# A three-mixer layer with its MLP: background weight sums paced by landed loads, and two gates moved into the first pair of the MLP

## The chip, the cores and the metric
The program runs on one core of a Trainium2 chip. The metric is device time in microseconds (us), the median of three runs. Lower is better.

## The reference, cut to what matters
One layer of a hybrid backbone for 512 latent and 128 context tokens of width 1024, all in fp32:

```
h = rms_norm(x, n1) * (1 + sc1) + sh1
h @ w_in                      -> three parallel mixers:
  A  windowed attention (8 heads, with a position bias)
  B  gated DeltaNet (4 heads, two directions)
  C  GLA (4 heads, two directions)
merged = sigmoid(m_a)*(o_a @ w_br[0]) + sigmoid(m_b)*(o_b @ w_br[1]) + sigmoid(m_c)*(o_c @ w_br[2])
x  = x + gt1 * (merged @ w_o)
h2 = rms_norm(x, n2) * (1 + sc2) + sh2
u_val, u_gate = split(dw_conv(h2 @ w_up, f_conv))     # depthwise, width 3, 2816 columns each
x  = x + gt2 * ((silu(u_gate) * u_val) @ w_down)
```

Outputs are the two token streams, the context's keys and values, and the final states of B and C.

## The kernel before, in words
The 640 tokens lie as columns, features in partitions. A product takes a 128-column tile of a weight matrix, splits it into a high and a low float32r part and makes three products (high by high, high by low, low by high). `plan` lists all weight tiles in the order of use. `W(key)` steps through it by an index `i`: it loads up to two entries ahead into a ring of three buffers `raw` (SP issues, L140 and L270), and splits one ahead (ScalarE copies to `wh`, L149, VectorE subtracts to `wl`, L150, two buffers each). Entries 0 to 39 are the input projections, 40 to 55 and 56 to 71 the merge columns and branch products of C and of B by turns (`m`, `br`), 72 to 79 the `m` of A, 80 to 87 its `br`, 88 to 95 `w_out`, 96 to 103 the plain up-projections of MLP tiles 0 to 3 (`uv` value, `ug` gate), then the rest of the MLP. While entries 40 to 79 are worked off, the turns of attention run between them: scores, bias, softmax and values.

**The weight sums.** MLP tiles 4 to 21 (blocks 1 to 5 of `FBLK`) are computed in pairs of half-products (`up_pair`), Strassen-like, which needs sums of quarter blocks of `w_up`. They are made by DMA alone, DRAM to DRAM with adding on the way: eight transfers for each block (`sum_steps`), each of 1 MB or 0.75 MB, 40 in all, issued by GpSimd (POOL) in program order (L250). POOL waits for a transfer on which the next one rests. In `W` one transfer is issued at each index of `STEP_AT`: 11 to 22, and 42 to 69. POOL also does small vector work: `rsq` (L344), moves of the solve in B (L968 to L998), the bias of attention scores (`bm`, L1413), and in the last branch product the sum that closes `merged` (L1310).

**Order.** Up to the MLP's pairs a scheduler sets each engine's order; in the pairs (`manual_schedule`) the order is that of the code for TensorE, VectorE and ScalarE.

**MLP.** Products of tile 0 and of `uv` 1 are made early. `up_tile(f)` does product, depthwise convolution (`conv`, L515 on ScalarE, four L517 on VectorE), `silu`, product with the value and split (`gated`). The calls are tiles 1, 2, 3, 0, between them `sums_h2(k)`, which makes and splits the sums of the right side (L1709 to L1712, L407, L408). Then 18 pairs: in `up_pair(f, dn)` the seven half-products of tile f go to PSUM tiles X, Y and Z; the gate of the tile before is finished between them (`prev`), and the down-products `dn` of the block before follow.

Of the kernel before, what the change touches and what calls it, by code (L numbers as in the profile page):

```python
# [58 lines left out]
def hybrid_step(ctx: ExitStack, tc: tile.TileContext, a: dict, o: list):  # L59
# [202 lines left out]
    STEP_AT = [*range(11, 23), *range(42, 42 + len(sum_q) - 12)]  # L262
# [32 lines left out]
    def W(key):  # L295
# [3 lines left out]
        if i in STEP_AT:  # L299
            sum_q.pop(0)()  # L300
# [3 lines left out]
        with tc.high_priority() if i else nullcontext():  # L304
# [1362 lines left out]
    def up_tile(f):  # L1667
        ys = {}

        for key, f2 in sorted((("uv", f), ("ug", NF + f)), key=lambda i: (i[0], f) in early):  # L1670
            ys[key] = ft()
            if (key, f) in early:
                src = early[key, f]
            else:
                w = W((key, f))
                if (key, f) == ("ug", 2):

                    ps = mtile(), mtile()
                    for k in range(KT):
                        for i, (ww, xx) in enumerate(((w[0], h2H), (w[0], h2L), (w[1], h2H))):  # L1680
                            for p_, cs in zip(ps, (L, R)):
                                PE.matmul(out=p_[:, :HALF], lhsT=ww[:, k, :], rhs=xx[:, k, cs],
                                          start=(k == 0 and i == 0), stop=(k == KT - 1 and i == 2))
                    src = ft()
                    for p_, cs in zip(ps, (L, R)):
                        S.copy(src[:, cs], p_[:, :HALF])
                    early[key, f] = src
                else:
                    ps = gtile()
                    gemm_b(ps, w, lambda k: h2H[:, k, :], lambda k: h2L[:, k, :], KT)  # L1690
                    src = body(ps)
                if (key, f) == ("ug", 3):
                    need_split(("st", f + 1, 0))
# [4 lines left out]
        fslots.extend(ys.values())  # L1698

# [22 lines left out]

    open_ = {}
    wds = [g[0] for g in plan if g[0][0] == "wd"]

    def up_pair(f, dn):
# [153 lines left out]
```

## Time and profile before

| | us |
|---|---|
| median of 3 runs | 1410.02 (1408.38 to 1410.82) |
| profiled execution | 1408.28 |
| its span | 1406.5 |
| TensorE busy | 1317.5 (94%) |
| VectorE busy | 878.7 (62%) |
| ScalarE busy | 575.9 (41%) |
| GpSimd busy | 204.1 (15%) |
| mean granted TensorE clock | 0.969 of full |

Busy times are sums over instructions; TensorE's are modelled at their ends. Idle time in brackets in a timeline row is what came before the instruction, with what ended it. A window's DMA share is the mean busy share of the core's 16 DMA engines.

### The profile page before, as it was taken

How to read it: one execution, taken by the hardware profiler on the slowest of the kernel's cores; microseconds unless marked ns; L12 is line 12 of the kernel's file. 1: busy time of each engine (PE TensorE's matmuls, PEld its weight loads, DVE VectorE, ACT ScalarE, POOL GpSimd, SP SyncE). 2: the span in 40 equal slices, each digit the busy share in tenths (PEclk: the TensorE clock that was granted, in tenths of full speed). 3: DMA queues.
4: the chain of work that ended last, by engine and by line, in shares of the span. 5: the costliest groups of instructions: out<-in, count | busy, mean ns of one | idle time of the engine just before them, and what ended most of it. 6: DMA issues, size and time to landing. Idle time of an engine off the chain costs nothing.

```text
span 1406.5 us, 26976 instructions
## 1 busy us (share of the span) xinstructions
PE 1317.5 (94%) x10985; PEld 1249.3 (89%) x10985; DVE 878.7 (62%) x1827; ACT 575.9 (41%) x1082; POOL 204.1 (15%) x228
## 2 busy tenths in 40 slices
PE   5999999998979895989999999999899999999998
PEld 4899889898868794978998889899799999999998
DVE  4675876775688752234333434457977777777784
ACT  4543324422575531133333332456544344443342
POOL 1011113402234322102332003210000000000000
PEclk9999999998989997999999999999899999999999
DMA  9624555733011149669885552522144334443424
GB/s 274 165 61 117 146 140 121 170 81 77 24 31 42 48 131 247 134 146 247 222 213 135 167 153 78 146 80 61 58 130 128 117 116 128 123 125 113 121 66 115
DMA packets 241359, 175.72 MB, mean 125 GB/s; under 512 B 22678, under 2 KB 226228, under 8 KB 241076
## 3 DMA queue, kind: packets, MB, share of 16 engines
q1 hardware_dynamic: 227571, 135.92, 34.7%
q0 software_dynamic: 13280, 37.75, 11.4%
q8 instruction: 87, 1.43, 0.4%
q10 hardware_dynamic: 384, 0.33, 0.1%
q14 instruction: 37, 0.30, 0.1%
HBM read 167.42 MB, written 44.30 MB: 151 GB/s over the span
## 4 chain that ended last, share of the span: by engine, by line
PE 75%; DVE 8%; DMA 5%; ACT 4%; POOL 3%; issue 2%; SPq 1%; ACTq 0%; POOLq 0%; DVEq 0%
PE g L374 41%; PE m L1735 11%; PE s L1735 5%; PE g L395 4%; DMA raw<-in_w_branch_dram 2%; PE s L622 2%; DMA wada<-in_w_ada_dram 1%; PE s L422 1%; DVE wl L150 1%; POOL ssn L344 1%; PE s L1448 1%; ACT wh L149 1%; DVE t L517 1%; PE s L1436 1%; PE m L1398 1%
## 5 line engine op out<-in xcount | busy, mean ns | idle before, releaser
L150 DVE TENSOR_TENSOR wl<-raw,wh 128x1024 fp32r<-128x1024 f32 (+1 forms) x176 | 193.1, 1097 | 199.9 <-ACT wh L149 190.4
L149 ACT CAST wh<-raw 128x1024 fp32r<-128x1024 f32 (+1 forms) x176 | 164.8, 944 | 301.2 <-PE g L374 168.5
L374 PE MATMUL g<-hH,wh 128*128 128x320 f32 x768 | 187.2, 323 | 11.7 <-ACT wh L149 10.1
L374 PE MATMUL g<-hL,wh 128*128 128x320 f32 x768 | 184.7, 319 | 0.6 <-DVE hL L470 0.6
L374 PE MATMUL g<-hH,wl 128*128 128x320 f32 x768 | 183.0, 317 | 0.0
L374 PEld LDWEIGHTS g<-hH,wh 128*128 128x128 f32 x768 | 129.4, 192 | 20.0 <-ACT wh L149 10.9
L374 PEld LDWEIGHTS g<-hL,wh 128*128 128x128 f32 x768 | 131.3, 192 | 3.2 <-issue 1.8
L374 PEld LDWEIGHTS g<-hH,wl 128*128 128x128 f32 x768 | 131.9, 192 | 2.0 <-issue 1.8
L374 PE MATMUL g<-r,whd 128*128 128x320 f32 x704 | 132.5, 310 | 1.1 <-DVE xa L1810 1.1
L374 PEld LDWEIGHTS g<-r,whd 128*128 128x128 f32 x704 | 110.4, 188 | 1.4 <-ACT t L1796 1.4
L1735 PE MATMUL m<-r,wh 128*128 128x320 f32 x432 | 96.7, 311 | 2.8 <-ACT r L407 1.8
L395 PE MATMUL g<-wh,hH 128*128 128x256 f32 x320 | 95.8, 299 | 3.4 <-DVE xb L730 3.4
L395 PE MATMUL g<-wl,hH 128*128 128x256 f32 x320 | 95.0, 297 | 0.0
L395 PE MATMUL g<-wh,hL 128*128 128x256 f32 x320 | 94.9, 296 | 0.0
L517 DVE SCALAR_TENSOR_TENSOR t<-t,fcols,t 128x127 f32<-128x127 f32 (+1 forms) x160 | 84.0, 548 | 10.3 <-ACT t L515 7.7
L374 PE MATMUL g<-r,wld 128*128 128x320 f32 x352 | 80.8, 311 | 1.0 <-DVE wld L150 1.0
L374 PE MATMUL g<-oz,wh 128*128 128x320 f32 x384 | 74.0, 314 | 6.1 <-ACT wh L149 4.9
L1735 PEld LDWEIGHTS m<-r,wh 128*128 128x128 f32 x432 | 72.3, 188 | 3.3 <-ACT r L407 2.1
L1810 DVE SCALAR_TENSOR_TENSOR xa<-g,modc,xa 128x512 f32<-128x512 f32 x96 | 48.4, 546 | 38.4 <-PE g L374 37.7
L395 PEld LDWEIGHTS g<-wh,hH 128*128 128x128 f32 x320 | 63.9, 200 | 5.2 <-DVE xb L730 3.6
L1735 PE MATMUL m<-r,wl 128*128 128x320 f32 x216 | 66.9, 310 | 0.0
L374 PEld LDWEIGHTS g<-oz,wh 128*128 128x128 f32 x384 | 60.1, 189 | 7.2 <-ACT wh L149 5.3
(602 smaller groups left out, 2881.4 us busy)
## 6 DMA issues: line engine op xcount, KB each, us to landing
raw<-in_w_in_dram SPq DMA_DIRECT2D x64, 512.0 KB
wsum<-in_w_up_dram POOLq DMA_DIRECT2D x18, 1024.0 KB, 10.8
raw<-wsum SPq DMA_DIRECT2D x72, 256.0 KB
wada<-in_w_ada_dram SPq DMA_DIRECT2D x32, 512.0 KB
raw<-in_w_up_dram SPq DMA_DIRECT2D x54, 256.0 KB
wsum<-in_w_up_dram POOLq DMA_DIRECT2D x12, 768.0 KB, 10.9
wat<-in_w_ada_dram SPq DMA_DIRECT2D x16, 512.0 KB
rawd<-in_w_down_dram SPq DMA_DIRECT2D x32, 256.0 KB
```

The source lines that it names most:

```text
L149: S.copy(wh[:, :m], raw[:, :m])
L150: V.tensor_sub(wl[:, :m], raw[:, :m], wh[:, :m].bitcast(F32))
L344: G.tensor_tensor(out=out, in0=out, in1=mh.broadcast_to([P, n]), op=ALU.pow)
L374: PE.matmul(out=ps[:, OFF + c0:OFF + c1], lhsT=ww[:, k, :], rhs=xx(k)[:, c0:c1], start=(k == 0 and i == 0), stop=(k == kt - 1 and i == 2))
L395: PE.matmul(out=ps[b][:, o:o + GRP], lhsT=xx[:, 4 * kh + k, cs], rhs=ww[:, k, :], start=(kh == 0 and c % 2 == 0 and k == 0 and i == 0), st ...
L422: PE.matmul(out=pa[32 * g:32 * g + 32, :w], lhsT=csil[:, k, :], rhs=t[g], start=start, stop=stop)
L517: V.scalar_tensor_tensor(out=y[:, o0:o1], in0=src[:, i0:i0 + o1 - o0], scalar=w3(t), in1=y[:, o0:o1], op0=ALU.mult, op1=ALU.add)
L622: PE.transpose(pt[:, i * P:(i + 1) * P], src[:, (c0 + i) * P:(c0 + i + 1) * P], ident)
L1398: PE.matmul(out=ps[:, 0:256], lhsT=qT_[t][b, qs], rhs=kT_[t][b, :TS].rearrange("p (r k) -> p r k", k=64)[:, :, CST[j]:CST[j] + 32], start= ...
L1436: PE.transpose(pt[:, i * P:(i + 1) * P], Pt[:, i * P:(i + 1) * P], ident)
L1735: PE.matmul(out=out, lhsT=ww[:, 4 * kh + k, :], rhs=xx(hl_, k), start=start and k == 0 and i == 0, stop=stop and k == 3 and i == 2, skip_g ...
L1810: V.scalar_tensor_tensor(out=x1[nt][:, c0:c1], in0=body(ps)[:, c0:c1], scalar=modc[:, 40 + nt, r:r + 1], in1=x1[nt][:, c0:c1], op0=ALU.mul ...
```

## The change
1. The 40 transfers of the sums are issued elsewhere. `SUM_AT` has 32 indices: 11 to 20, every second from 44 to 78, then 82, 86, 90 and 94. The last eight (block 5) are issued one in each of the first eight pairs.
2. Ahead of each transfer POOL copies one element of the `raw` buffer of that index to `tick`. POOL so waits until that load has landed, and the buffer can be loaded anew only after the copy.
3. Gate of tile 3 and both convolutions, gate and splits of tile 0 are taken out of `up_tile` and put into the first pair, as a list `gates`, between its half-products. `up_tile(3)` keeps the convolution of its value; the gate's product stays in PSUM until the pair.
4. Down-products of block 0 take their tiles in the order 1, 2, 3, 0.
5. The rest of the diff gives names to pieces that were there (`up_plain`, `gate_conv`, `gate_mul`, `gate_split` in place of `last_gate`).

```diff
-    STEP_AT = [*range(11, 23), *range(42, 42 + len(sum_q) - 12)]
+    SUM_AT = [*range(11, 21), *range(44, 80, 2), 82, 86, 90, 94]
+    tick = cp.tile([1, 1], F32, name="tick")
+    def sum_step(raw):
+        if sum_q:
+            G.tensor_copy(out=tick, in_=raw[0:1, 0:1])
+            sum_q.pop(0)()
...
-        if i in STEP_AT:
-            sum_q.pop(0)()
...
+        if i in SUM_AT:
+            sum_step(loaded[i])
         return split[i]
...
+        first = f == fst[1]
         u1, u2 = ft(), ft()
+        gates = open_.pop("gates", [])
...
+        if gates:
+            gate_conv(gates[0])
...
         V.tensor_add(u2[:, R], u2[:, L], Z)
+        if first:
+            gates[1][1] = conv_u(gates[1][1], gates[1][0])
         prod(X, w, 1, lambda j, k: hH2[j][:, 4 + k, L], False, True)
+        if gates:
+            gate_mul(gates[0])
...
         need_split(("st", f, 3))
+        sum_step(loaded[pidx["st", f, 3]])
...
+        if first:
+            V.tensor_sub(u2[:, R], Y, u2[:, R])
+            need_split(dn[0])
+            gate_conv(gates[1])
+            gate_mul(gates[1])
+        for g in gates:
+            gate_split(g)
...
+               ks=None if b else (1, 2, 3, 0))
...
-    up_tile(3)
+    y3 = ft()
+    conv(y3, up_plain("uv", 3), lambda tap: fcols[:, tap, 3:4])
     sums_h2(3)
-    up_tile(0)
+    open_["gates"] = [[3, y3, up_plain("ug", 3)], [0, early["uv", 0], early["ug", 0]]]
+    need_split(("st", fst[1], 0))
```

What this makes of the order on POOL where the turns of attention begin, before:

```order
L1371 MEMSET bm 128x1152
L250 DMA wsum_96<-wsum_95 16x16384
L250 DMA wsum_100<-wsum_99 16x16384
L1413 TENSOR_TENSOR bm<-Gt,wm 128x256 x2
L250 DMA wsum_96<-in_w_up_dram 512x512
L250 DMA wsum_100<-in_w_up_dram 512x512
L1413 TENSOR_TENSOR bm<-Gt,wm 128x256 x2
L250 DMA wsum_102<-in_w_up_dram 512x512
L250 DMA wsum_105<-in_w_up_dram 512x512
```

and now (`raw_6318` and `raw_6443` are the loads of entries 44 and 46, `raw_6587` that of 48):

```order
L1380 MEMSET bm 128x1152
L1422 TENSOR_TENSOR bm<-Gt,wm 128x256 x7
L268 COPY tick<-raw_6318 1x1
L250 DMA wsum_95<-in_w_up_dram 512x512
L268 COPY tick<-raw_6443 1x1
L250 DMA wsum_99<-in_w_up_dram 512x512
L1422 TENSOR_TENSOR bm<-Gt,wm 128x256 x2
L268 COPY tick<-raw_6587 1x1
L250 DMA wsum_96<-wsum_95 16x16384
```

Eight transfers stood ahead of the eighth `bm`; now two do, each behind a `tick`, and from there on two `bm` stand between one `tick` and the next or the one after.

The same queue in the last branch product, where each row of L1310 closes `merged` for one of eight tiles. Before, nothing stood between them:

```order
L1310 TENSOR_TENSOR xa_504<-xa_504,xb_516 128x640
L1310 TENSOR_TENSOR xb_524<-xb_524,xb_530 128x640
L1310 TENSOR_TENSOR xb_512<-xb_512,xb_527 128x640
L1310 TENSOR_TENSOR xa_505<-xa_505,xb_518 128x640
L1310 TENSOR_TENSOR xb_513<-xb_513,xb_522 128x640
```

and now (`raw_9450` is the load of entry 86, `raw_9639` that of 90):

```order
L1319 TENSOR_TENSOR xa_505<-xa_505,xb_517 128x640
L268 COPY tick<-raw_9450 1x1
L250 DMA wsum_108<-wsum_107 16x12288
L1319 TENSOR_TENSOR xb_525<-xb_525,xb_531 128x640
L1319 TENSOR_TENSOR xb_513<-xb_513,xb_528 128x640
L1319 TENSOR_TENSOR xa_506<-xa_506,xb_519 128x640
L1319 TENSOR_TENSOR xb_514<-xb_514,xb_523 128x640
L1319 TENSOR_TENSOR xb_512<-xb_512,xb_527 128x640
L268 COPY tick<-raw_9639 1x1
L250 DMA wsum_104<-in_w_up_dram 512x512
L1319 TENSOR_TENSOR xa_503<-xa_503,xb_518 128x640
```

A copy of a sum now stands between the second and the third tile, an adding transfer ahead of the eighth.

VectorE around the start of the first pair, before (`gx` rows make the last right sides, `t<-g` rows are convolutions of tile 3 out of PSUM, L1750 is the pair's first combination):

```order
L150 TENSOR_TENSOR wl_10808<-raw_10694,wh_10807 128x1024
L517 SCALAR_TENSOR_TENSOR t_9579<-g_10758,fcols,t_9579 128x511
L1709 TENSOR_TENSOR gx_9910<-gx_9910 128x320
...
L408 TENSOR_TENSOR r_9597<-gx_9910,r_9596 128x640
L408 TENSOR_TENSOR r_9599<-gx_10212,r_9598 128x640
L408 TENSOR_TENSOR r_9595<-t_9582,r_9594 128x640
...
L517 SCALAR_TENSOR_TENSOR t_9583<-t_9580,fcols,t_9583 128x511
L517 SCALAR_TENSOR_TENSOR t_9583<-t_9580,fcols,t_9583 128x127
L150 TENSOR_TENSOR wl_10881<-raw_10755,wh_10880 128x1024
L517 SCALAR_TENSOR_TENSOR t_9583<-t_9580,fcols,t_9583 128x127
L1750 TENSOR_TENSOR t_9584<-t_9582,m_10865 128x320
```

and now:

```order
L1718 TENSOR_TENSOR gx_9933<-gx_9933 128x320
L150 TENSOR_TENSOR wl_10845<-raw_10720,wh_10844 128x1024
L1719 TENSOR_TENSOR gx_9933<-gx_9933,gx_10237 128x320
L150 TENSOR_TENSOR wl_10882<-raw_10793,wh_10881 128x1024
L1720 TENSOR_TENSOR gx_10237<-gx_10237,gx_9933 128x320
L417 TENSOR_TENSOR r_9616<-gx_9933,r_9615 128x640
...
L526 SCALAR_TENSOR_TENSOR t_9604<-g_10792,fcols,t_9604 128x511 x2
L417 TENSOR_TENSOR r_9618<-gx_10237,r_9617 128x640
L526 SCALAR_TENSOR_TENSOR t_9604<-g_10792,fcols,t_9604 128x127 x2
L1780 TENSOR_TENSOR t_9600<-t_9602,m_10867 128x320
```

The eight rows of L517 that convolve tile 0 have left this stretch, and the second weight split of the pair stands ahead of the last right sides. Behind the pair's second combination there now stand eight convolution rows, two gate products and two splits in place of one product and one split.

## Rows read from the trace of the kernel before

**Rows 1.** The page: an engine's busy time.
```profile
PE 1317.5 (94%) x10985; PEld 1249.3 (89%) x10985; DVE 878.7 (62%) x1827; ACT 575.9 (41%) x1082; POOL 204.1 (15%) x228
```

**Rows 2.** Windows: start, end, length; busy us (instructions) by engine; clock, DMA share, GB/s.
```profile
525.00:560.00 35.00, 18.91 (x120) 15.12 (x118) 10.76 (x29) 6.09 (x14) 9.74 (x13) 0.79 0.95 257
665.00:700.00 35.00, 35.00 (x269) 33.10 (x268) 13.33 (x33) 12.22 (x27) 11.47 (x12) 1.00 0.91 246
542.00:556.00 14.00, 1.51 (x5) 1.03 (x4) 1.81 (x3) 1.28 (x3) 1.40 (x2) 0.61 0.88 311
556.00:570.00 14.00, 12.24 (x56) 11.03 (x57) 1.20 (x3) 2.20 (x5) 0.00 (x0) 0.66 0.37 108
```

**Rows 3.** DMA view of 520 to 560: packets, MB, share; issues, KB each, us to landing.
```profile
q0 software_dynamic: 2039, 7.28, 62.6%
q1 hardware_dynamic: 3317, 3.38, 31.0%
...
wsum<-in_w_up_dram POOLq DMA_DIRECT2D x4, 1024.0 KB, 13.7
```

**Rows 4.** Timeline of POOL, 520 to 560: start, length, instruction, count.
```profile
528.31 2.12 POOL L250 DMA_DIRECT2D wsum<-in_w_up_dram  x2
...
538.31 1.49 POOL L250 DMA_DIRECT2D wsum<-in_w_up_dram  x2
...
541.32 1.24 POOL L250 DMA_DIRECT2D wsum<-in_w_up_dram  x2
```

**Rows 5.** Timeline of SP's issues, 520 to 560.
```profile
525.25 0.86 SPq L140 DMA_DIRECT2D raw<-in_w_in_dram  x1
```

**Rows 6.** Timeline of ScalarE, 520 to 560.
```profile
549.85 1.04 ACT L149 CAST wh<-raw 128x1024 fp32r<-128x1024 f32 x1 [7.61 <-DMA raw<-in_w_in_dram]
```

**Rows 7.** Timeline of TensorE, 540 to 606.
```profile
550.95 0.90 PE L374 MATMUL g<-hH,wh 128*128 128x320 f32 x2 [8.88 <-ACT wh L149]
...
557.24 1.43 PE L374 MATMUL g<-oz,wh 128*128 128x320 f32 x4 [4.86 <-ACT wh L149]
...
602.05 1.28 PE L1448 MATMUL s<-PT,Vj 128*64 128x128 f32 x7 [5.08 <-ACT PT L1438]
```

**Rows 8.** Chain of waits over the span: start, length, what; two turns.
```profile
662.47 7.23 PE g L374 x48
...
676.11 7.23 PE g L374 x48
```

**Rows 9.** Timeline of TensorE, 140 to 158.
```profile
148.23 1.30 PE L1209 MATMUL s<-ident,xa 128*128 128x128 f32 x5 [1.14 <-DVE stmp L980]
```

**Rows 10.** Timeline of POOL: the solve of B; the last branch product.
```profile
187.62 1.45 POOL L998 COPY T<-XT 32x320 f32<-32x320 f32 x3 [4.80 <-DMA XT<-Xd]
...
857.15 1.95 POOL L1310 TENSOR_TENSOR xa<-xa,xb 128x640 f32<-128x640 f32 x1 [2.43 <-DVE xb L1309]
...
879.07 2.41 POOL L1310 TENSOR_TENSOR xb<-xb,xb 128x640 f32<-128x640 f32 x1 [2.49 <-DVE xb L1309]
```

**Rows 11.** Timeline of TensorE, 885 to 892.
```profile
890.52 1.33 PE L622 MATMUL s<-ident,t 128*128 128x128 f32 x5 [1.17 <-DMA t<-in_x_sample_dram]
```

**Rows 12.** Chain of waits, at the loads of x_sample.
```profile
885.41 5.06 DMA t<-in_x_sample_dram
```

**Rows 13.** Windows at the start of the pairs, and of a later pair.
```profile
990.00:1000.00 10.00, 10.00 (x71) 10.00 (x70) 10.00 (x19) 6.78 (x11) 0.00 (x0) 1.00 0.10 29
1000.00:1010.00 10.00, 9.07 (x61) 8.54 (x59) 9.70 (x19) 5.54 (x9) 0.00 (x0) 1.00 0.18 52
1010.00:1020.00 10.00, 4.48 (x13) 3.46 (x14) 9.16 (x16) 4.46 (x7) 0.00 (x0) 0.63 0.10 30
1020.00:1030.00 10.00, 10.00 (x59) 9.79 (x59) 6.51 (x10) 5.45 (x9) 0.00 (x0) 0.85 0.55 161
1040.00:1060.00 20.00, 20.00 (x137) 20.00 (x137) 15.49 (x26) 8.81 (x14) 0.00 (x0) 1.00 0.41 119
```

**Rows 14.** Timeline of VectorE, 1005 to 1035.
```profile
1028.77 2.19 DVE L517 SCALAR_TENSOR_TENSOR t<-t,fcols,t 128x511 f32<-128x511 f32 x4 [0.36 <-ACT t L515]
```

More of the change, by code (lines that the diff above doesn't have):

```diff
@@ L364, in hybrid_step, with gemm_p @@
     V.tensor_copy(cols[:, :16], pt[:, :16])
-    def gemm_p(ps, w, xh, xl, kt, step=2, more=0):
+    def gemm_p(ps, w, xh, xl, kt, step=2, more=0, ks=None):
         wh, wl = w
-        for k in range(kt):
-            if k and k % step == 0:
+        ks = ks or range(kt)
+        for n, k in enumerate(ks):
+            if n and n % step == 0:
                 yield
@@ L374, in gemm_p @@
                     PE.matmul(out=ps[:, OFF + c0:OFF + c1], lhsT=ww[:, k, :], rhs=xx(k)[:, c0:c1],
-                              start=(k == 0 and i == 0), stop=(k == kt - 1 and i == 2))
+                              start=(n == 0 and i == 0), stop=(n == kt - 1 and i == 2))
     def gemm_b(*args, **kw):
@@ L1673, in up_tile @@
                 src = early[key, f]
-            else:
[L1675 to L1693, printed above, removed]
+            elif (key, f) == ("ug", 2):
+                w = W((key, f))
+                ps = mtile(), mtile()
+                for k in range(KT):
+                    for i, (ww, xx) in enumerate(((w[0], h2H), (w[0], h2L), (w[1], h2H))):
+                        for p_, cs in zip(ps, (L, R)):
+                            PE.matmul(out=p_[:, :HALF], lhsT=ww[:, k, :], rhs=xx[:, k, cs],
+                                      start=(k == 0 and i == 0), stop=(k == KT - 1 and i == 2))
+                src = early[key, f] = ft()
+                for p_, cs in zip(ps, (L, R)):
+                    S.copy(src[:, cs], p_[:, :HALF])
+            else:
+                src = up_plain(key, f)
             conv(ys[key], src, lambda tap, f2=f2: fcols[:, tap, f2:f2 + 1])
@@ L1721, in conv_u, with gate_conv, gate_mul, gate_split @@
         return y
+    def gate_conv(g):
+        f, _, u = g
+        y = ft()
+        conv(y, u, lambda tap: fcols[:, tap, NF + f:NF + f + 1])
+        if f != 3:
+            fslots.append(u)
+        g[2] = y
+    def gate_mul(g):
+        S.activation(out=g[2], in_=g[2], func=AF.Silu)
+        V.tensor_mul(g[1], g[1], g[2])
+        fslots.append(g[2])
+    def gate_split(g):
+        ac[g[0]] = rt(2)
+        split_x(g[1], *(t[:, :T] for t in ac[g[0]]))
+        fslots.append(g[1])
     open_ = {}
@@ L1786, in up_pair @@
             if f == NF - 1 and i < 3:
[L1787 removed]
+                (gate_conv, gate_mul, gate_split)[i](open_["gates"][0])
             down(*key[1:])
             need_load(*wds[wds.index(key) + 2:wds.index(key) + 3])
[L1791 to L1800 removed]
     def down(b, nt):
```

36 lines of the change are left out of this document (10 added, 26 removed).

## The prediction

> **What bounds the kernel now.** I read the page first. TensorE is busy for 94% of the span, so time is won only where it idles or runs slowly [rows 1]. Then windows of equal length. Between 525 and 560 TensorE works 18.91 of 35 us, with the DMA engines at 0.95. Between 665 and 700 they are nearly as full (0.91), and TensorE works all 35 us [rows 2]. So full DMA engines alone do not stop it; what stops it is a load that lands too late.
>
> The DMA view of 520 to 560 says who filled them. The sums' queue (q0) takes 62.6% of 40 us, 25.0 us for 7.28 MB, and all other loads (q1) 31.0%, 12.4 us for 3.38 MB; four 1 MB sums took 13.7 us (median) to land [rows 3]. POOL issued six sums there, two at each of 528.31, 538.31 and 541.32 [rows 4]. The weight load of entry 42 was issued at 525.25 [rows 5], and ScalarE, which waited for it, began its copy at 549.85 [rows 6]: 24.6 us for 512 KB. TensorE stood 8.88 us for that copy, 4.86 us for the one after, and 5.08 us more at 602 behind a copy that also waited for its load [rows 7].
>
> **Term 1, the sums spaced out.** The six sums issued from 528 to 542 are gone from there: in the new order seven `bm` stand first, and the two sums then let through each follow a landed load, of entries 44 and 46. By the rates above, the loads of this stretch need 12.4 us of DMA time, and get it from 525 on; the load of entry 42 is then down well before TensorE is through with its earlier work at 542. What can go:
> - idle time, 8.88 + 4.86 + 5.08 = 18.8 us [rows 7];
> - slow work. The granted clock is 0.66 in the window from 556, so about 0.34 / 0.5 = 0.68 of its 14 us, 9.5 us, were at 1.2 GHz and not at 2.4, some 8 of them busy; with the 1.51 us of the window before, 9.4 us ran at half speed [rows 2] after TensorE had stood idle for 8.88 us. Half of that, 4.7 us, goes.
>
> Together 23.5 us. Slow work after the wait at 602 is not counted; I set it against waits that may stay. From above the term is 26 us, if that goes too and is half as long as the slow work counted. From below it is half, 12 us, if one sum in flight slows a load half as much as several do.
>
> From entry 44 on, a sum starts on every second entry, once in a turn of 676.11 - 662.47 = 13.6 us [rows 8], where before it was two. Between 665 and 700 those two and all loads moved 246 GB/s, 3.4 MB a turn, and TensorE never stood [rows 2]; with one sum of 1 MB less, 3.4 us less of DMA time at 25.0 / 7.28 us per MB, no new wait is counted.
>
> The Trainium skill speaks against this part: its page "DMA: Bandwidth & Descriptors", section "Rules for kernel authors", advises to issue a DMA early, compute, and wait for it late. By that, holding the sums back wins nothing, and the sum below would be 23.5 us higher. The trace disagrees for this stretch [rows 3, 5 to 7]: transfers needed only in the MLP were issued early, and loads needed at once came late.
>
> **Term 2, the sums' new places.** POOL works in order, so each `tick` holds what is behind it until a load has landed. Three places bear on the path.
> - Entry 14's `tick` stands before the second `rsq` of the keys. There TensorE waits 1.14 us already [rows 9]. 0 us if that load has landed by then; 3.4 us if the DMA time of one sum lies ahead of it. I take 1.
> - Ten sums now run up to entry 20, where before half of them came later. The solve's exchange through DRAM is among them: POOL's copies of `XT` wait 4.80 us for it [rows 10]. 0 to 4 us if a hop or two become half as long again; I take 2.
> - In the last branch product the chain runs through POOL: each L1310 takes 1.95 us and then waits 2.43 us for VectorE, which waits for ScalarE, which waits for the L1310 [rows 10]. The copy of a sum between the second and the third tile can wait for the load of entry 86, 0.5 us (0 to 2). The adding transfer ahead of the eighth tile fits into the 2.49 us gap, since issuing takes some 1.06 us [rows 4, 10]. But it runs into the loads of `x_sample`, for which TensorE waits 1.17 us [rows 11] and which is 5.06 us of the chain [rows 12]. It adds 3.4 us of DMA time beside them: 0 to 4 us, I take 2.5.
>
> The eight sums in the MLP cost nothing: POOL has no other work there, and a pair's window shows DMA at 0.41 of 20 us [rows 13], to which 0.75 MB adds 2.6 us. Block 5 is needed ten tiles later. Should that cover go, a pair would wait for about one landing, 13.7 us [rows 3]. The 40 `tick` copies themselves are of one element; I count them at nothing, since POOL idles 85% of the span.
>
> Term 2 costs 6.0 us, between 0 and 14.
>
> **Term 3, the gates.** VectorE is full from 990 (10.00, 9.70 and 9.16 of 10 us), and TensorE stands 0.93 + 5.52 = 6.45 us between 1000 and 1020 [rows 13]. It then runs slowly: granted 0.63 and 0.85 mean 7.4 and 3 us at 1.2 GHz. All of the 3 and about 3.5 of the 7.4 are busy, so 3.2 us are lost. At most 9.7 us can go.
>
> Tile 0's two convolutions leave that stretch, 2.19 us each [rows 14]. They come back inside the pair, with a gate product and splits, some 6 us more of VectorE work between the pair's first combination and the end of its half-products. TensorE has four half-products there, 48 matmuls, 7.2 us at the pace of the plain ones [rows 8], then a down-product whose last two tiles need exactly these gates. I followed both engines through the pair: the left side's last split comes out at most 1 us earlier than now, the second weight split some 8 us earlier, so the half-products end about 7 us earlier; the first down-product then waits for the splits of tiles 3 and 0 for about 2 us. That leaves 5 us, of which I take 4.5. VectorE, with 15.49 us of work in 20 us of a later pair [rows 13], catches up in the next one. From above 9.7; from below a loss of 4 us, if the 6 added us of VectorE come on the path with no earlier start. The order 1, 2, 3, 0 puts the late tiles last; alone it costs nothing, since the products are the same.
>
> **Sum.** 1408.28 - 23.5 + 6.0 - 4.5 = 1386.3 for the profiled execution. That lies 1.7 us under the median of 1410.02, so I expect a median of 1388.
>
> **Rivals.**
> - *A sum in flight slows the loads, however few there are.* In 520 to 560 the loads got half the time that the sums got [rows 3]. If each sum still delays the load behind it, half of term 1 stays and term 2 is nearer 8: 1410.0 - 12 + 8 - 4.5 = 1401.5. Against it: 665 to 700 [rows 2]. The page "DMA: Bandwidth & Descriptors", section "Queues, rings and completion order" of the Trainium skill has each DMA engine go round among its queues by packets; by that one queued sum takes as large a share as six, though for a shorter time. Chance 0.17.
> - *The first pair becomes VectorE's.* Term 3 turns into 4 us of loss: 1396.5. For it: 6 us of work more beside 7.2. Against it: TensorE was already waiting on that engine before. Chance 0.10.
> - *The `tick` becomes the new wait, and the kernel slower.* Behind each of the 18 `tick` of entries 44 to 78 stands `bm`, without which no turn of attention goes on, and the `raw` buffer is free only after it. This decides if a load takes longer than one turn, 13.6 us, to land; 24.6 us did occur [rows 5, 6]. Then some 2 us a turn in 16 turns, 32 us, outweigh 23.5 + 4.5 - 6.0: about 1420. Against it: that landing had six sums beside it, and now has one. Chance 0.05.
> - *The change does not space anything.* Loads run two entries ahead, so a `tick` can find its load landed and pass at once; the sums then bunch as before and the loads wait, with term 3 eaten by term 2: 1410. Against it: between `tick` pairs stand `bm` rows that go by turns. Chance 0.05.
>
> **The numbers.** The forecast, 1388, has the remaining 0.63. About 0.2%, 2.8 us, is what a measurement of this kernel tells from no change. The first two rivals are faster too: faster 0.90, same 0.05, slower 0.05. For the range, the forecast's own bounds give 1410.0 - 26 + 1 - 9.7 = 1375 below; above, the first rival with term 2 a little dearer, 1404. That leaves the last two rivals and a tail below outside.
>
> **What would show it.** Right: in the window of 35 us after the first `bm` TensorE is busy for more than 32 us at a clock near 1.00; no copy of ScalarE waits over 3 us for a `raw` load in entries 42 to 56; sums are about 13 us apart on POOL; at the start of the pairs TensorE idles for under 4 us. Term 2 is wrong if TensorE's wait for `x_sample` stays at 1.2 us, or grows beyond 5. The whole is wrong if `bm` waits for a `tick`, or if TensorE still waits for `wh` for over 10 us in all.

## The result, and the profile after

The changed kernel takes 1393.9 us, the median of four runs (1386.24 to 1396.34), beside 1409.2 us for the kernel before on the same chip: 0.989 of it, with a 95% interval of 0.985 to 0.9925. A second set of six runs, below, gave 1391.9 us and 0.990 (0.9875 to 0.993). The profiled execution took 1386.24 us, the fastest of its set.

The page, its line of busy times and the line of the sums' queue: TensorE has 9.6 us less busy time than in [rows 1], a share of 94% as before.

```profile
PE 1307.9 (94%) x10985; PEld 1241.0 (90%) x10985; DVE 877.2 (63%) x1827; ACT 575.7 (42%) x1082; POOL 211.1 (15%) x268
...
q0 software_dynamic: 13280, 37.75, 12.2%
```

The windows that answer to [rows 2]:

```profile
525.00:560.00 35.00, 32.01 (x215) 28.08 (x213) 14.35 (x35) 10.32 (x20) 6.35 (x9) 0.95 0.48 120
...
542.00:556.00 14.00, 11.80 (x71) 9.79 (x71) 5.46 (x17) 3.63 (x10) 2.50 (x5) 0.88 0.48 131
556.00:570.00 14.00, 14.00 (x100) 13.39 (x99) 4.72 (x7) 4.53 (x7) 2.41 (x4) 1.00 0.75 170
```

From 525 to 560 TensorE now works 32.01 us in place of 18.91, at a granted clock of 0.95 in place of 0.79, and the DMA engines are half empty. POOL's timeline in that stage answers to [rows 4]. Each row gives start, length, instruction, and in brackets the idle time before it and what ended it:

```profile
555.09 0.18 POOL L268 COPY tick<-raw 1x1 f32<-1x1 f32 x1 [9.72 <-DMA raw<-in_w_in_dram]
555.33 1.16 POOL L250 DMA_DIRECT2D wsum<-in_w_up_dram  x1
567.77 0.17 POOL L268 COPY tick<-raw 1x1 f32<-1x1 f32 x1 [11.28 <-DMA raw<-in_w_in_dram]
568.21 1.04 POOL L250 DMA_DIRECT2D wsum<-in_w_up_dram  x1 [0.27 <-issue]
```

One sum is issued at 555 and the next 13 us later, where six were issued from 528 to 542. But TensorE has new waits. The list of its waits over the span (us in total, times, longest):

```profile
PE m L1029 <- DMA XT<-Xd: 10.1, 2, 9.9
...
PE s L631 <- DMA t<-in_x_sample_dram: 5.7, 1, 5.7
...
PE g L383 <- ACT wh L149: 1.8, 2, 1.2
```

In the kernel before, the same list had

```profile
PE g L374 <- ACT wh L149: 15.0, 3, 8.9
```

The wait for `x_sample` was 1.17 us [rows 11], and those for `XT` were 0.4 us each; in exchange the 15.0 us for `wh` are down to 1.8. The next table is the main instrument of what follows; the kernels of its lower rows are explained below. It cuts the profiled execution of each kernel at the same ten instructions of TensorE, found in the timelines by their order. In the kernel before these lie at 161.1, 206.6, 527.5, 662.5, 772.6, 832.8, 891.9, 984.4, 1048.5 and 1397.6 us. Lengths in us; some 10.5 us follow the last.

| kernel | S1 start | S2 exchange of `XT` in B | S3 to the first merge product | S4 attention, merge of C | S5 merge of B | S6 `m` of A, first `br` | S7 last branch product, `x_sample` | S8 `w_out`, plain tiles | S9 first pairs | S10 rest |
|---|---|---|---|---|---|---|---|---|---|---|
| before | 161.1 | 45.5 | 320.9 | 135.0 | 110.2 | 60.2 | 59.0 | 92.6 | 64.1 | 349.1 |
| changed | 157.9 | 55.2 | 317.8 | 109.9 | 110.2 | 61.3 | 63.6 | 92.5 | 59.3 | 347.9 |
| again | 161.1 | 56.3 | 318.4 | 109.4 | 110.2 | 61.6 | 63.6 | 92.2 | 59.4 | 347.9 |
| sums_only | 162.4 | 55.9 | 318.2 | 111.2 | 110.2 | 61.6 | 63.5 | 91.6 | 63.9 | 349.1 |
| gates_only | 159.6 | 45.2 | 323.9 | 134.4 | 110.2 | 60.2 | 57.4 | 90.4 | 58.5 | 347.9 |
| xt_clear | 160.6 | 44.1 | 325.0 | 111.3 | 110.2 | 61.3 | 62.9 | 92.1 | 58.7 | 347.9 |
| xs_clear | 158.5 | 57.2 | 319.5 | 111.1 | 110.2 | 61.9 | 58.1 | 90.4 | 58.9 | 347.9 |
| no_tick | 159.8 | 45.1 | 321.1 | 114.2 | 110.2 | 65.9 | 58.9 | 90.4 | 59.1 | 347.9 |
| old_places | 158.2 | 57.0 | 316.1 | 128.1 | 113.1 | 60.2 | 57.3 | 90.4 | 58.6 | 347.9 |
| twice | 158.1 | 57.1 | 314.6 | 125.7 | 119.7 | 60.2 | 63.4 | 91.2 | 58.9 | 347.9 |
| clear_places | 157.6 | 44.4 | 322.6 | 111.2 | 110.2 | 61.4 | 57.8 | 91.2 | 58.9 | 347.9 |
| clear_late_tick | 161.1 | 45.3 | 317.3 | 111.3 | 110.2 | 61.1 | 57.8 | 91.4 | 64.4 | 347.9 |
| clear_mlp_tick | 159.7 | 45.2 | 320.6 | 111.3 | 110.2 | 61.7 | 58.1 | 90.9 | 58.7 | 348.0 |
| clear_no_tick | 157.3 | 46.7 | 322.6 | 113.6 | 110.2 | 67.3 | 57.2 | 90.5 | 63.6 | 347.9 |

Read the first two rows against each other: the change wins 25.1 us in S4, 4.8 in S9, 1.2 in S10, 3.2 in S1 and 3.1 in S3. It loses 9.7 in S2, 1.1 in S6 and 4.6 in S7. The sum is -22, the difference of the profiled times.

My theory after this: the gain of S4 is that of the sums spaced out; the losses of S2 and S7 are sums that now fly beside transfers on which TensorE waits at once. The rivals: those two waits have other causes; the wait for a landed load, and not the place, wins or loses; a sum slows loads however few there are.

### The profile page after: what moved, and what is told of

It reads as the page before. It is cut to its first block, busy times and chain, and to the rows that moved or that the text cites. A ratio compares the mean times of both kernels' runs of the same rounds, so it can differ in the third digit from the quotient of the medians.

```text
span 1384.5 us, 27048 instructions
## 1 busy us (share of the span) xinstructions
PE 1307.9 (94%) x10985; PEld 1241.0 (90%) x10985; DVE 877.2 (63%) x1827; ACT 575.7 (42%) x1082; POOL 211.1 (15%) x268
## 4 chain that ended last, share of the span: by engine, by line
PE 63%; DVE 7%; ACT 3%; POOL 3%; DMA 2%; issue 2%; SPq 0%; ACTq 0%; DVEq 0%; POOLq 0%
PE g L383 37%; PE m L1763 11%; PE s L1763 5%; PE s L431 1%; PE s L631 1%; PE g L404 1%; DVE wl L150 1%; PE s L1457 1%; PE s L1445 1%; POOL ssn L352 1%; DMA raw<-in_w_in_dram 1%; DMA t<-in_x_sample_dram 1%; PE m L1407 1%; POOL xb L1319 1%; PE m L1691 1%
## 5 line engine op out<-in xcount | busy, mean ns | idle before, releaser
L383 PEld LDWEIGHTS g<-hH,wh 128*128 128x128 f32 x768 | 128.7, 190 | 11.8 <-issue 3.9
L383 PEld LDWEIGHTS g<-r,whd 128*128 128x128 f32 x704 | 110.2, 188 | 2.1 <-ACT t L1742 1.4
L526 DVE SCALAR_TENSOR_TENSOR t<-t,fcols,t 128x511 f32<-128x511 f32 (+1 forms) x160 | 84.3, 548 | 10.4 <-ACT t L524 7.7
L404 PEld LDWEIGHTS g<-wh,hH 128*128 128x128 f32 x320 | 63.5, 199 | 5.2 <-DVE xb L739 3.6
L268 POOL COPY tick<-raw 1x1 f32<-1x1 f32 x40 | 8.4, 211 | 369.8 <-DMA raw<-in_w_up_dram 181.7
```

Source lines behind the costliest of these rows:

```text
L404: PE.matmul(out=ps[b][:, o:o + GRP], lhsT=xx[:, 4 * kh + k, cs], rhs=ww[:, k, :], start=(kh == 0 and c % 2 == 0 and k == 0 and i == 0), st ...
L526: V.scalar_tensor_tensor(out=y[:, o0:o1], in0=src[:, i0:i0 + o1 - o0], scalar=w3(t), in1=y[:, o0:o1], op0=ALU.mult, op1=ALU.add)
```

## Experiments: do the two parts, and the two new waits, come from where I think

**again** is the changed kernel itself.

> The changed kernel, unchanged, to see how far its runs lie apart. Theory: its executions lie between 1386 and 1397 us with a median near 1394, 0.988 to 0.990 of the kernel before. The profile shows again a wait of TensorE for XT (5 to 10 us) and for x_sample (4 to 6 us), and no wait for wh in entries 42 to 56. Rival: these two waits are chance and at least one of them is under 2 us in this profile; then the sums' new places did not cause them.

Measured: 1391.9 us (1387.0 to 1398.9). The profiled run took 1390.7 us. Both waits are there again; that for `XT` has split in two:

```profile
PE m L1030 <- DMA XT<-Xd: 6.2, 1, 6.2
...
PE s L631 <- DMA t<-in_x_sample_dram: 5.3, 1, 5.3
...
PE m L1029 <- DMA XT<-Xd: 3.3, 2, 3.1
```

So they are no accident. From the first profile this one differs by 4.5 us, of which 4.3 arise in S1 and S2; after that the two run in step. The expectation held for both waits; two of the six executions took longer than the 1397 us that I had named. What makes the executions of this kernel differ by 12 us in all was not tried.

**sums_only** has the sums of the changed kernel, and the gates as before: `up_tile(3)` and `up_tile(0)` whole, `prev` and `last_gate` in the pairs. Against the kernel before its edit is

```
-    STEP_AT = [*range(11, 23), *range(42, 42 + len(sum_q) - 12)]
+    SUM_AT = [*range(11, 21), *range(44, 80, 2), 82, 86, 90, 94]
...
-        if i in STEP_AT:
-            sum_q.pop(0)()
...
+        if i in SUM_AT:
+            sum_step(loaded[i])
...
         need_split(("st", f, 3))
+        sum_step(loaded[pidx["st", f, 3]])
```

> The sums' places and the tick of the changed kernel, the gates as before. Theory: the gates are worth 4.8 us of the change (from 968.47 to 1027.77 the changed kernel took 59.3 us, the one before 64.1), so this is 4.8 us slower than the changed kernel, about 1398.5, 0.992 of the kernel before, and the stretch from the first product of tile 4 to the downs of the second pair takes 64 us again. Rival: TensorE gives the gain back later in the MLP, where VectorE has to catch up: under 2 us apart.

Measured: 1394.3 us, 0.992 (0.990 to 0.993). S9 is 63.9 us, as before, and S10 349.1: against the changed kernel's 59.3 and 347.9 the gates are worth 5.8 us in the traces. The medians of this set lie only 2.4 us apart, less than the runs of one kernel do; the stretches carry the size, the medians only the direction.

**gates_only** is the other half: the changed kernel with the sums as before.

```
-    SUM_AT = [*range(11, 21), *range(44, 80, 2), 82, 86, 90, 94]
+    STEP_AT = [*range(11, 23), *range(42, 42 + len(sum_q) - 12)]
...
+        if i in STEP_AT:
+            sum_q.pop(0)()
...
-        if i in SUM_AT:
-            sum_step(loaded[i])
...
-        sum_step(loaded[pidx["st", f, 3]])
```

> The kernel before with the gates of tiles 3 and 0 in the first pair, the sums as before. Theory: the two parts don't touch each other, so the stretch from the first product of tile 4 to the downs of the second pair takes 59.3 us in place of 64.1 and the time falls by 4.8 us: 0.9966 of the kernel before. Rival: with the sums of block 1 long complete either way, nothing else can differ; but if the first pair waits for a split of a sum's load in this order, it is under 2 us.

Measured: 1398.5 us, 0.994 (0.992 to 0.9965). S4 stays at 134.4, S9 falls to 58.5 and S10 to 347.9: 6.8 us by these two stretches. The interval puts the whole at 5 to 12 us, more than I expected; S7 and S8 were 3.8 us shorter too in this execution, by 1.6 of them in S7, where the gates touch nothing. In the stretches the two parts are independent: S4 belongs to the sums, S9 and S10 to the gates. The medians do not add up as well: 11.9 us for the sums alone and 8.3 for the gates alone stand beside 14.3 for both, a difference at the edge of what the intervals allow.

**xt_clear** moves five sums.

```
-    SUM_AT = [*range(11, 21), *range(44, 80, 2), 82, 86, 90, 94]
+    SUM_AT = [*range(11, 16), *range(21, 26), *range(44, 80, 2), 82, 86, 90, 94]
```

> The changed kernel with the five sums of entries 16 to 20 moved to entries 21 to 25, where the DMA engines are busy for 0.13 of the time. Theory: the sums in flight slow the hops of Xd and XT through DRAM; without them the wait of 9.9 us at XT falls below 3 us, the products behind it come 6 to 7.6 us earlier, and 3 to 6 us of that are left at the end: about 1389.5, 0.9855 of the kernel before. Rival: the wait is that of VectorE's chain ahead of Xd, the sums have nothing to do with it: wait and time stay, 1394. A second rival: the new places cost the same in the stretch of entries 21 to 25, since POOL works for the states there and the tick holds it up: the wait goes, the time stays.

Measured: 1382.6 us, 0.983 (0.981 to 0.9845), 9 us better than the changed kernel by the medians, where I had 3 to 6. The profiled executions lie closer: this one is 6.1 us shorter than that of the repeat and 1.7 shorter than the first, so a part of the 9 us has no place in the traces. The wait at `XT` is gone and S2 is 44.1 us in place of 55.2. What a sum does to the exchange is in SP's issues. `XT` can be loaded only when `Xd` has landed in DRAM. In the changed kernel:

```profile
176.58 0.31 SPq L997 DMA_DIRECT2D Xd<-Y  x1
177.75 0.31 SPq L998 DMA_DIRECT2D Xd<-Uw  x1
184.26 0.32 SPq L1006 DMA_DIRECT2D XT<-Xd  x1
```

With the sums moved away:

```profile
178.84 0.31 SPq L997 DMA_DIRECT2D Xd<-Y  x1
180.02 0.31 SPq L998 DMA_DIRECT2D Xd<-Uw  x1
181.21 0.32 SPq L1006 DMA_DIRECT2D XT<-Xd  x1
```

The hop of 160 KB held the next one up for 7.7 us from its issue beside the sums, and for 2.4 without them. From 165 to 205 the sums' queue has a share of 57.9% in the changed kernel, and 5.8% here. The packets show how the delay comes about. In the changed kernel, from 177 to 182:

```profile
q0 software_dynamic: 374, 0.76, 82.4%
q1 hardware_dynamic: 375, 0.38, 28.5%
```

The two queues take turns, packet for packet. Those of q1 hold 1 KB here, while the hops', seen alone in xt_clear, hold 3.6 KB (0.27 MB in 76). So by their size they belong to the weight load issued ahead of the hop in the same queue: the sum slows that load, and the hop stands behind it.

The second rival has a part in it as well. S3 is 7.2 us longer than in the changed kernel. A part of that is slack: S3 is 314 to 320 us long in the kernels that have waited in S2, and 317 to 325 in the others. But some 4 us arise in one place, at the two sums of entries 24 and 25. In POOL's timeline their `tick` waits stand in front of the keys' `ssn`,

```profile
265.76 0.17 POOL L268 COPY tick<-raw 1x1 f32<-1x1 f32 x1 [1.28 <-DMA raw<-in_w_in_dram]
266.19 0.57 POOL L250 DMA_DIRECT2D wsum<-wsum  x1 [0.26 <-issue]
266.77 2.02 POOL L352 TENSOR_TENSOR ssn<-ssn,mh 128x10 f32<-128x10 f32 x1
```

and VectorE stands for it:

```profile
268.83 0.83 DVE L1207 TENSOR_TENSOR xa<-xa,ssn 128x640 f32<-128x640 f32 x1 [2.97 <-POOL ssn L352]
```

**xs_clear** leaves out the two last entries of the list, so two more sums fall to the MLP.

```
-    SUM_AT = [*range(11, 21), *range(44, 80, 2), 82, 86, 90, 94]
+    SUM_AT = [*range(11, 21), *range(44, 80, 2), 82, 86]
```

> The changed kernel without the sums of entries 90 and 94; all later sums move by two, and ten run in the MLP in place of eight. Theory: the sum issued at 861 us slows the loads of x_sample that start at 865; without it TensorE's wait of 5.7 us for x_sample falls to about 1.2 us, as before, and the time by 4.5 us: 1389.5, 0.9855 of the kernel before. The two more sums in the MLP cost nothing. Rival: the loads of x_sample compete with the w_out loads and not with the sum: the wait stays above 4 us, the time at 1394.

Measured: 1383.2 us, 0.9835 (0.982 to 0.985), nearly 9 us better than the changed kernel where I had 4.5. In the chain of waits the changed kernel has

```profile
864.91 9.62 DMA t<-in_x_sample_dram
```

and this one

```profile
871.71 4.07 DMA t<-in_x_sample_dram
```

The landing of 256 KB took 9.62 us beside a sum issued at 861.05, and 4.07 without; TensorE's wait fell by 5.5 us, and so did S7. Another 2.1 us are in S8, and there the clock differs. Windows of 17 us before and after the end of the wait, in the changed kernel

```profile
858.00:875.00 17.00, 8.93 (x53) 7.91 (x54) 8.26 (x15) 3.45 (x4) 6.00 (x4) 0.87 0.86 214
875.00:892.00 17.00, 17.00 (x103) 17.00 (x102) 5.66 (x7) 6.97 (x13) 2.83 (x3) 0.83 0.35 102
```

and in this one

```profile
858.60:875.60 17.00, 14.04 (x88) 12.59 (x86) 10.31 (x18) 5.93 (x8) 6.88 (x3) 1.00 0.62 180
876.00:893.00 17.00, 17.00 (x121) 16.99 (x121) 8.20 (x10) 8.68 (x17) 1.58 (x1) 1.00 0.49 143
```

Behind the longer wait TensorE worked all 17 us at a mean granted clock of 0.83, and did 103 instructions where it did 121 here. So a loss beyond the length of the wait went with it. That the wait caused it is not shown: in the kernel before the clock is 0.84 from 891 to 908 behind a wait of only 1.17 us, and S8 is as long, 92.6; in no_tick, below, it is 1.00 from 875 to 892 behind one of 1.7 us. The two more sums in the MLP cost nothing (S9 58.9, S10 347.9).

## Experiments: the wait for a landed load, and the rate

**no_tick** takes the copies away, and with them the wait.

```
         if sum_q:
-            G.tensor_copy(out=tick, in_=raw[0:1, 0:1])
             sum_q.pop(0)()
```

> The changed kernel without the copies of one element, so that no sum waits for a landed load; the sums stand at the same entries. Theory: in the attention stage the places do the work, since a bm of the turn stands between two sums on POOL; two sums start together at the beginning of it, then one a turn, and the 25 us that the stretch from 527.5 to 640.8 gained are lost by at most 5. In the first phase sums start earlier without the copies, so the wait at XT changes: below 6 us if they are through by then. Total 1385 to 1395, 0.985 to 0.992 of the kernel before. Rival: the wait for a landed load is what frees the loads; then TensorE waits for wh again for over 8 us and the stretch loses over 10: 1403 or more, 0.997.

Measured: 1382.7 us, 0.982 (0.9785 to 0.986): faster than the changed kernel by some 9 us, a little more than I expected of the theory. The stretches show a gain and a loss. S2 is 45.1 and S7 58.9; the wait at `XT` is gone, and that for `x_sample` is 1.7 us. A sum that reads no load is put by the scheduler behind other work of POOL, and so the sums happened to miss both places (two at 194.41, after the exchange; one at 860.06, 8.9 us ahead of the load of `x_sample`, and the next at 887.89). But S4 is 4.3 and S6 4.6 us longer. At the start of the attention stage three sums come close together,

```profile
523.10 1.16 POOL L250 DMA_DIRECT2D wsum<-in_w_up_dram  x1
...
536.79 1.00 POOL L250 DMA_DIRECT2D wsum<-in_w_up_dram  x1
...
540.42 0.56 POOL L250 DMA_DIRECT2D wsum<-wsum  x1
```

and where the merge of A begins the sums of 753.67, 754.20 and 760.15 do. There the chain of waits reads

```profile
760.93 12.69 DMA raw<-in_w_in_dram
```

The copy is thus worth some 9 us where the weight loads set the pace. It brings a wait for a landed load and another order on POOL; these two were not told apart. And the copy was not the reason for the losses of S2 and S7 as such: it only decided where those sums fell.

**old_places** keeps the wait and goes back to the entries of the kernel before.

```
-    SUM_AT = [*range(11, 21), *range(44, 80, 2), 82, 86, 90, 94]
+    SUM_AT = [*range(11, 23), *range(42, 42 + len(sum_q) - 12)]
```

> The changed kernel with the entries of the kernel before (11 to 22 and 42 to 69, two sums a turn), each with the wait for a landed load. On POOL six copies, of the loads of entries 42 to 47, stand ahead of the eighth bm. Theory: two sums a turn leave the DMA engines room, since from 665 to 700 TensorE worked all the time beside them, but bm now stands behind the load of entry 47; it costs 3 to 15 us of the 25: 1396 to 1408. Rival 1: the wait for the landed load is all that matters, wherever the sums stand: within 3 us of the changed kernel. Rival 2: the copies hold bm up so far that the turn stands: over 1410, slower than the kernel before, with TensorE waiting behind bm for over 20 us in all.

Measured: 1399.3 us, 0.995 (0.992 to 0.997). S4 and S5 are 21 us longer than in the changed kernel, more than I had allowed; S6 and S7 are 7 us shorter, as this list has no sums there. My reason, `bm` behind the copies, explains little of it: after the copies `bm` mostly waits on for VectorE's `mx`, 2.8 to 7.5 us from 610 to 661; at 580.47 and in some later turns it follows them at once and can have cost a part. What surely waits is ScalarE for the loads, and TensorE for `PT`, which stands behind that copy on ScalarE. From 525 to 700:

```profile
ACT wh L149 <- DMA raw<-in_w_in_dram: 69.1, 7, 15.2
...
PE s L1457 <- ACT PT L1447: 10.6, 3, 6.2
```

**twice** was made to tell rate from order: two sums a turn from entry 44 on, with fewer copies ahead of `bm`.

```
-    SUM_AT = [*range(11, 21), *range(44, 80, 2), 82, 86, 90, 94]
+    SUM_AT = [*range(11, 21), *range(44, 62), 82, 86, 90, 94]
```

> The changed kernel with its sums of entries 44 to 78 at every entry from 44 to 61, so two a turn in place of one, each with its wait for a landed load; nine bm stand ahead of them on POOL in place of seven and at most four copies ahead of the next, not six. Theory: the rate decides. With two sums a turn the DMA engines hold some 0.85 in the stretch from 560 to 665, ScalarE's copies wait for their raw loads for 40 us or more in all (69 in the run with the old places, 16 in the changed kernel), and PT behind them on ScalarE holds TensorE: 10 to 20 us slower than the changed kernel, 1402 to 1412. Rival: in the run with the old places it was the copies ahead of bm that cost; then this loses under 6 us: 1392 to 1398.

Measured: 1410.8 us, 1.0025 (1.001 to 1.004): the whole gain is gone, at the upper end of what I had expected of the theory. S4 and S5 are 15.8 and 9.5 us longer than in the changed kernel. ScalarE again waits 69.9 us in seven pieces for its loads. The reason can be followed through one turn. POOL and SP here:

```profile
650.77 0.17 POOL L268 COPY tick<-raw 1x1 f32<-1x1 f32 x1 [9.93 <-DMA raw<-in_w_in_dram]
651.26 1.03 POOL L250 DMA_DIRECT2D wsum<-in_w_up_dram  x1 [0.32 <-issue]
651.91 1.17 POOL L268 COPY tick<-raw 1x1 f32<-1x1 f32 x1
653.03 0.64 POOL L250 DMA_DIRECT2D wsum<-in_w_up_dram  x1
...
666.54 0.17 POOL L268 COPY tick<-raw 1x1 f32<-1x1 f32 x1 [6.50 <-DMA raw<-in_w_in_dram]
```

```profile
654.70 0.37 SPq L140 DMA_DIRECT2D raw<-in_w_in_dram  x1
```

and in the changed kernel:

```profile
645.15 0.17 POOL L268 COPY tick<-raw 1x1 f32<-1x1 f32 x1 [1.67 <-DMA raw<-in_w_in_dram]
645.60 0.65 POOL L250 DMA_DIRECT2D wsum<-in_w_up_dram  x1 [0.28 <-issue]
...
658.29 0.17 POOL L268 COPY tick<-raw 1x1 f32<-1x1 f32 x1 [1.73 <-DMA raw<-in_w_in_dram]
```

```profile
653.66 0.37 SPq L140 DMA_DIRECT2D raw<-in_w_in_dram  x1
```

In the changed kernel the sum starts when a load has landed, 8.1 us before the next load is issued (653.66 - 645.60), and that load lands within 4.6 us (658.29 - 653.66). With two sums the landing of the load frees both, the copy on ScalarE starts at the same moment, and the next load is issued 3.4 us after the first sum and 1.7 after the second: it lands after 11.8 us (666.54 - 654.70). (A load of `wada` of 512 KB stands ahead of it in its queue too, issued 1.6 us before it here and 3.5 in the changed kernel.) In the changed kernel no packet of a sum is left when the load is issued. In twice, from 660 to 664, the sums are still under way:

```profile
q0 software_dynamic: 405, 0.62, 87.8%
q1 hardware_dynamic: 409, 0.21, 26.6%
```

Again the queues move equal numbers of packets, and with its smaller packets the load gets a quarter of the bytes. So a landed load is a good signal for one sum, which fits into the gap, and a bad one for two, which start right ahead of the next load. It also says why two sums a turn did no harm in the kernel before from 665 to 700. There POOL issued them behind the load of the turn, and not ahead of it; SP and POOL in that kernel:

```profile
675.32 0.37 SPq L140 DMA_DIRECT2D raw<-in_w_in_dram  x1
```

```profile
677.52 2.09 POOL L250 DMA_DIRECT2D wsum<-in_w_up_dram  x2
```

That is read from the two traces; a kernel with two sums a turn behind the load was not tried.

**clear_places** puts together what the first experiments taught: none of the sums beside the exchange, none ahead of `ssn`, none in the last branch product.

```
-    SUM_AT = [*range(11, 21), *range(44, 80, 2), 82, 86, 90, 94]
+    SUM_AT = [*range(11, 16), 21, 22, 23, 26, 27, *range(44, 80, 2)]
```

> The changed kernel with the sums of entries 16 to 20 at entries 21, 22, 23, 26 and 27, and those of 82, 86, 90 and 94 in the MLP, twelve in place of eight. Theory: both waits go, that for XT (9.3 us in the run that moved these five sums) and that for x_sample (8.8 us in the run without 90 and 94), and the ssn of POOL at 266 and 276 us, which the copies of entries 24 and 25 held up for 2.0 and 1.5 us, start at once: 1391.9 - 9.3 - 8.8 - 3.5 = 1370, between 1368 and 1376, 0.971 to 0.979 of the kernel before. Rival: the waits are replaced by others of the same size, or twelve sums in the MLP collide with the loads of the pairs: 1380 or more.

Measured: 1371.1 us (1368.6 to 1377.3), 0.975 (0.972 to 0.978), the number that the three effects had given, and the fastest version of all: some 36 us below the kernel before and 21 below the changed one (12 to 17 us between the profiled executions). S2 is 44.4 and S7 57.8, S4 and S9 keep their gains. The line of busy times:

```profile
PE 1307.2 (95%) x10985; PEld 1239.6 (90%) x10985; DVE 876.2 (64%) x1827; ACT 575.8 (42%) x1082; POOL 212.0 (15%) x268
```

**clear_late_tick**, **clear_no_tick** and **clear_mlp_tick** ask, on top of it, where the wait is needed. The first has it from entry 44 to the end of the list of entries, and neither earlier nor in the MLP:

```
         if sum_q:
-            G.tensor_copy(out=tick, in_=raw[0:1, 0:1])
             sum_q.pop(0)()
...
         if i in SUM_AT:
+            if i >= 44:
+                G.tensor_copy(out=tick, in_=loaded[i][0:1, 0:1])
             sum_step(loaded[i])
```

> The version with the moved places (1371 us), without the wait for a landed load in entries 11 to 27, with it from 44 on. Theory: in the first phase only the place counts, and a sum without the copy is put behind POOL's work of that time, clear of the XT hops: the same within 4 us, 1367 to 1375, with no wait for XT over 3 us. Rival: five sums in a row now stand ahead of the clearing of T and of kd, and an adding transfer waits on POOL for the one it adds to (10.4 us in the run without copies): TensorE then waits behind kd, 4 to 10 us slower.

Measured: 1378.5 us, 0.980 (0.978 to 0.983), so the rival came out in size, but not in its place. S1 was 3.5 us longer than in clear_places, the sums in a row at 195 to 207 added at most 2, and all of it was back by 350; S2 and S3 together are 4.4 us shorter. The loss is in S9, 64.4 in place of 58.9: my edit had also taken the wait out of the MLP, and POOL issued the twelve sums of that part from 927 to 979. ScalarE then waited for the first load that reads a sum, and TensorE for ScalarE:

```profile
990.10 1.04 ACT L149 CAST wh<-raw 128x1024 fp32r<-128x1024 f32 x1 [8.15 <-DMA raw<-wsum]
```

```profile
991.19 0.56 PE L1764 MATMUL m<-r,wh 128*128 128x320 f32 x2 [3.70 <-ACT wh L149]
```

The next has the wait nowhere:

```
         if sum_q:
-            G.tensor_copy(out=tick, in_=raw[0:1, 0:1])
             sum_q.pop(0)()
```

> The version with the moved places, without any wait for a landed load, in the attention stage too. Theory: there the copy is worth something, since without it three sums started within 17 us at the beginning of the stage and the stretch from 527 to 775 lost 9.3 us: 4 to 10 us slower than the run before it in this list, about 1378. Rival: the places alone do it, under 2 us apart: 1371.

Measured: 1387.8 us, 0.986 (0.984 to 0.989), 9.3 us slower than clear_late_tick, as the theory had it. It is S4 (2.3 us) and S6 (6.2 us), the two places at which no_tick had lost. The last has the wait from entry 44 on and in the MLP:

```
         need_split(("st", f, 3))
+        G.tensor_copy(out=tick, in_=loaded[pidx["st", f, 3]][0:1, 0:1])
         sum_step(loaded[pidx["st", f, 3]])
```

> The run clear_late_tick with the wait for a landed load in the MLP again, so that only entries 11 to 27 go without it. There twelve sums were issued from 927 to 979 us, the first load of sums for tile 4 landed late (ScalarE waited 8.15 us for it, TensorE 3.70), and 5.3 us were lost by 994, while the 4.5 us lost at 206 were back by 350. Theory: the twelve sums in a bunch are the whole loss; with a sum a pair it is gone: 1378.5 - 5.4 = 1373, within 4 us of the version that waits everywhere (1371). Rival: the loss comes from the first phase after all: 1377 to 1380.

Measured: 1375.1 us, 0.978 (0.976 to 0.980). S9 is back at 58.7. The median fell by 3.4 us where I had 5.4, and lies 4 above clear_places, whose interval overlaps with this one; whether the wait is worth anything in entries 11 to 27 stays open.

## Why the prediction was right, and where not

The forecast was 1388 us; the two sets gave 1393.9 and 1391.9, inside the range, and faster than before. Two terms held and one failed. The 2.8 us that the prediction took for the least change to be told from none was too little: six executions of the changed kernel span 12 us, and 22 of the kernel before 16.5.

*Term 1* (-23.5 us) was right in its place and reason, and 1.6 us too small: S4 fell from 135.0 to 109.9 us. The three waits of [rows 7] left 1.16 us, that of 550.95. The slow windows of [rows 2] went from granted 0.61 and 0.66 to 0.88 and 1.00. Of the gain some 4 us hang on the copy (no_tick), the rest on the places; the copies at the old places won 6.9 us of it (old_places). One of my signs was false: I said that no copy of ScalarE would wait over 3 us for a load in entries 42 to 56, and two did, at 567.75 for 7.92 us and at 581.14 for 7.95; TensorE still had other work. And one reading behind it does not carry: from the window of 665 to 700 [rows 2] I took that full DMA engines alone do not stop TensorE. In twice a DMA share of 0.86 to 0.89 went with 10.5 us of idle time of TensorE between 560 and 665. The share does not tell whether a load lands in time.

*Term 2* (+6.0 us) is the term that was mis-sized; it measured 9.1 to 14.3 us. The sums' new places cost 6.6 us in S2 and S3, 1.1 in S6 and 4.6 in S7, together 12.3, or 9.1 with the 3.2 that S1 was shorter; by the repeat, which has no such gain in S1, it is 14.3. Its steps:
- Entry 14's `tick` at the second `rsq`, +1: S1 lies between 157.3 and 162.4 over all kernels, with and without the wait there. No effect can be seen.
- The exchange of `XT`, 2 us between 0 and 4, "if a hop or two become half as long again". This step failed. A hop became three times as long, 7.7 us in place of 2.4, since the sums had most of the DMA time there (57.9% to 36.8%) and the hop stood behind a weight load that they slowed; S2 lost 9.7 us, of which S3 gave 3.1 back. The mechanism was named and its price taken too low.
- `x_sample`, 2.5 us between 0 and 4: 4.6, past the bound, and the wait of 5.7 us past the 5 that I had set as proof against the term. The 0.5 us for the copy between the second and the third tile cannot be seen: S7 is no longer than the wait grew. The DMA time of one sum that I had counted, 3.4 us, was less than the 5.5 us by which the landing grew.
- The eight sums of the MLP, 0 us: right, and the wait is not the reason: in no_tick the eight go out from 937 to 972 without it, and S9 is 59.1. Only the twelve of clear_late_tick and clear_no_tick, without it, cost 5 us there.

*Term 3* (-4.5 us) was right: S9 fell by 4.8 us, and S10, which I had not counted, by 1.2. The first of these is seen where [rows 13] showed TensorE idle for 6.45 of 20 us, from 1000 to 1020; the same stretch, which begins some 16 us earlier, now reads

```profile
984.10:994.10 10.00, 9.03 (x60) 8.51 (x58) 9.82 (x18) 5.30 (x9) 0.00 (x0) 1.00 0.30 100
994.10:1004.10 10.00, 8.23 (x44) 8.00 (x45) 8.37 (x15) 5.28 (x8) 0.00 (x0) 0.83 0.35 104
```

with 2.74 us idle, and a clock of 0.83 where it was 0.63.

The *sum* met the profiled execution to 0.1 us by chance: term 2 was some 3 to 6 us too cheap, terms 1 and 3 and the short S1 made up for it. In the repeat, whose S1 is that of before, term 2 is 8.3 us dearer than forecast, and terms 1 and 3 give 2.1 and 1.4 us more: 4.8 us, and its median lies 3.9 above 1388.

*The rivals.* That a sum slows the loads however few there are falls for one sum a turn (S4 at 109.9, a load down in 4.6 us), since that sum is through before the next load, and holds for two (twice). It holds for a single sum too where that is in flight beside the load, as at `x_sample` (9.62 us in place of 4.07); so its second half, term 2 nearer 8, came true. Its page in the Trainium skill, "DMA: Bandwidth & Descriptors", section "Queues, rings and completion order", has each DMA engine take turns among its queues by packets. The traces agree: 374 packets of the sums and 375 of the loads in 5 us at the exchange, 405 and 409 in 4 us of twice. From 165 to 205 a packet of the sums holds 3.2 KB (5.24 MB in 1632) and one of the other loads 0.47 KB (3.62 MB in 7660), so equal turns leave the loads few bytes. The first pair did not become VectorE's. The `tick` as a new wait came true in xt_clear only, in front of `ssn`, and for 4 us; in the changed kernel one `bm` (568.87) stood directly behind a `tick`, which I had named as a sign against the whole, but TensorE was busy all the time from 556 to 570. And the sums are spaced, one in 13 us. The rule "issue early, wait late" of the same page of the Trainium skill, section "Rules for kernel authors", would have had the spacing win nothing: clear_no_tick, which issues as early as the order lets it, lost 16.7 us against clear_places. For a transfer whose result is due much later than its neighbours', these runs disagree with it.

## What to carry to other kernels

Transfers that only have to be done some time belong into gaps of the transfers that are waited for: look up the loads' issue and landing times, give each gap one such transfer that fits, and start it by the landing of a load, so that the order on the issuing engine alone does not let them bunch up. Before placing one, look for the short transfers in a chain (an exchange through DRAM, a first load of a stage) and keep it clear of them, and clear of path work on the engine that issues it. A mean DMA share tells neither.

## What the runs showed of the hardware that I had not expected

- A load of 512 KB landed in 4.6 us with one 1 MB DRAM-to-DRAM transfer started 8 us ahead of it, and in 11.8 us with two of 0.75 MB started 3.4 and 1.7 us ahead. A hop of 160 KB went from 2.4 to 7.7 us. While both queues had packets to move they moved equal numbers of them, 374 and 375 from 177 to 182 in the changed kernel, 405 and 409 from 660 to 664 in twice, whatever their size. At `x_sample` it was otherwise: from 865 to 867 the sums' queue moved 190 packets and the loads' 72; why was not found.
- After a wait of 5.7 us TensorE worked 17 us without a pause at a mean granted clock of 0.83, and at 1.00 after one of 0.2 us; but also at 0.84 after one of 1.17 us (the kernel before) and at 1.00 after one of 1.7 us (no_tick). The length of the wait alone does not tell the clock behind it.
- A one-element copy ahead of a transfer also moves it in the scheduler's order. Taking the copy away removed the wait at `XT` and cut that for `x_sample` from 5.7 to 1.7 us, though the copy's own wait had not caused them.
